# A hybrid encoder step: third weight buffer one trunk later, and the second half's MLP operands read whole from DRAM

## The chip, the cores and the metric

The kernel runs on one core of a Trainium2 chip. The metric is the device time of one execution in microseconds; the time before is the median of three runs. Five engines work side by side, each through its own list of instructions in order: PE (TensorE, matrix products), DVE (VectorE), ACT (ScalarE), POOL (GpSimd), and SP (SyncE), which here issues nearly all transfers (DMAs). An instruction that waits for a semaphore holds up everything behind it on its engine.

## The reference

One inference step of one layer of a streaming encoder with d = 1024, for 1024 prompt tokens and 32 sample tokens, all in float32:

```
h = rms_norm(x);  q,k,v,ch,cb,cc,ga,gb = split(h @ w_in)
a = window_attention(q,k,v) @ w_attn_out
b = (cb * conv3(cc * ch)) @ w_conv_out
x = x + (sigmoid(ga) * a + sigmoid(gb) * b) @ w_mix_out
x = x + memory_attention(rms_norm(x) @ w_cq) @ w_co        # 4 heads of 64, 256 memory rows
x = x + relu(rms_norm(x) @ w_up)**2 @ w_down               # hidden 4096
y = rms_norm(x)
```

The outputs are y, the last keys and values, the convolution's state and the memory keys and values.

## The kernel before, in words

Activations lie with features on the 128 partitions, in 8 blocks (f = 0 to 7), and tokens along the free axis. The 1056 tokens are cut into three chunks of 384, 384 and 288 (`CH`). A float32 product is made of three faster ones: each operand is split into a rounded high part and the remainder, and `gemm` (L193 to L195) adds wh·hi, wh·lo and wl·hi, 24 matmuls for a weight tile of 128x1024. `product` (L864 to L866) does the same for half a tile.

*Weights.* The program is a plan of items, each with the weight it needs. `fetch_w` (L155) issues the load of a raw tile on SP into one of two buffers named wr; if the dictionary `third` is filled, every third load goes to a buffer of another pool, so that three are in turn (the pool with tag ws behind the gate stage). `issue_w` then splits the tile: ACT casts it to wh (L129), DVE subtracts to get wl (L130). Items ask for their weights two ahead (`LOOK`). For the odd tiles of w_conv_out, w_mix, w_cq and w_co, which all three chunks use, wl is stored to DRAM as wl_d when first made (L172) and loaded back later (L166), so that only the cast is repeated.

*Stages around the change.* In the attention and gate stages POOL makes sums of weights in the tiles of the pool with tag ws and in xacc (`sum_step`: loads at L712, additions at L719, stores to gsum_d, wsum_d and usum_d at L723 and L725). `after_gates` (L1018) ends the gate stage; there `third` is filled. Then comes the trunk of each chunk: 8 items of w_conv_out (`do_conv_out`, L1042) and 8 of w_mix (`do_mix`, L1057). The first trunk carries one item more, the second trunk's first. The second trunk runs beside the first chunk's cross-attention, which uses w_cq, w_co and the memory keys (mkr, L1076). The third trunk is mixed with the MLP's first products.

*The MLP.* It works on halves of 528 tokens, and its `up` products on quarters of 264. `up_one(i, q)` (L1313) makes one product pair a and b of quarter q; the first half of the 24 matmuls goes to a, ACT copies a out of its accumulator (L1324), the second half goes to b, and DVE empties b (L1327, L1328). `put` and `flush` send the results to s_d and b_d (L1310). The operands of quarter 1 lie in `xa[1]`, in eight tiles named Z that `open_first` (L1221) opens; quarter 1 spans tokens 264 to 527, thus 120 tokens of the first chunk and 144 of the second. `normed(c, f)` (L1277) makes block f of chunk c of the MLP's normalised input in a ct buffer (there are six), and stores it to xn_d in DRAM (L1282). `second_split(f)` splits Z in place: ACT casts (L1296), DVE subtracts (L1297). `chunk_col` and `chunk_row` make the row R of scales for a chunk (DVE L240, PE L241 and L242, ACT L252), which the query products need when DVE takes them from their accumulators (L1109).

*What sets the order.* The list of fillers (`ones_q`, trunk items) and the table `at`, filled by `then(i, ...)`, say after which filler each call stands. The order on each engine is made by a scheduler from that program; only what is marked with `pin` keeps its place. So a DMA can be lifted far ahead of its place in the text, as far as its buffer allows in the scheduler's reckoning.

Of the kernel before, what the change touches and what calls it, by code (L numbers as in the profile page):

```python
# [10 lines left out]
F32 = mybir.dt.float32  # L11
# [11 lines left out]
CH = [(0, 384), (384, 384), (768, 288)]  # L23
NF = 8
HT = 528
QT = 264
# [14 lines left out]
def hybrid_step(ctx: ExitStack, tc: tile.TileContext, io):  # L41
    nc = tc.nc
    act, dve, pool_e, pe, sp = nc.scalar, nc.vector, nc.gpsimd, nc.tensor, nc.sync
# [7 lines left out]
    def opened(name, **kw):  # L51
        cm = tc.tile_pool(name=name, **kw)
        return cm, cm.__enter__()

    def closed(cm):
        cm.__exit__(None, None, None)
# [17 lines left out]
    def col(j):  # L74
        return prm[:, j : j + 1]
# [6 lines left out]
    xn_d = dram.tile([P, NF, NT], F32, name="xn_d")  # L82
# [14 lines left out]
    def pin(ins):  # L97
        return tc.keep_in_program_order(ins)
# [6 lines left out]
    def tmp(n, dt=F32):  # L105
        return tp.tile([P, n], dt, tag="ct", bufs=NCT, name=nm("ct"))
# [11 lines left out]
    def item(fn, *keys):  # L118
        plan.append((fn, keys))
        worder.extend(keys)  # L120
# [24 lines left out]
    third = {}  # L145
# [68 lines left out]
    def xacc_tile():  # L214
        xacc[0] = tp.tile([P, 1056], F32, tag="xacc", name=nm("xacc"))
        return xacc[0]
# [37 lines left out]
    def chunk_stats(c):  # L254
        chunk_col(c)
        chunk_row(c)
# [19 lines left out]
    W = {}  # L276
# [490 lines left out]
    def yslot(c):  # L767
        return slot(Y[c if c < 2 else "top"], f"Y{c}", CH[c][1])
# [22 lines left out]
    def pump(n):  # L791
        for into, at, t, get in coming:
            hi, lo = into[at] = (get(), get())
            pin(act.copy(hi, t))
            pin(dve.tensor_sub(lo, t, hi.bitcast(F32)))
        coming.clear()
        for into, at, src, cols, get in wanted[:n]:
            t = cols() if callable(cols) else tmp(cols)
            sp.dma_start(t, src)
            coming.append((into, at, t, get))  # L800
        del wanted[:n]
# [216 lines left out]
    def after_gates():  # L1018
        nonlocal m_cm, mpool, cr_cm, cr
        assert not pieces and "new" not in W  # L1020
        closed(x_cm)
        xacc_tile()
        third.update(n=0, pool=W["pool"])
        m_cm, mpool = opened("mpool", bufs=18, reuse_waits="tile")
        cr_cm, cr = opened("cross", bufs=1, reuse_waits="tile", side="right")

    item(after_gates)


# [73 lines left out]
    def do_cq(c, j):  # L1103
        def fn(w):
            n = CH[c][1]
            a = acc_tile([P, n])
            gemm(a, w, xc[c])
            t = tmp(n)
            dve.scalar_tensor_tensor(t, a, 0.125, R[c], op0=ALU.mult, op1=ALU.mult)  # L1109
            for e in range(2):  # L1110
                own, other = slice(64 * e, 64 * e + 64), slice(64 - 64 * e, 128 - 64 * e)
                q = yslot(c)
                act.copy(q[own], t[own])
                dve.tensor_sub(q[other], t[own], q[own].bitcast(F32))
                qc[2 * j + e, c] = q

        return fn
# [75 lines left out]
    def do_co(c, half):  # L1193
        def fn(w):
            n = CH[c][1]
            wh, wl = w
            fs = range(4 * half, 4 * half + 4)
            for f in fs:
                a = acc_tile([P, n])
                for k in range(2):  # L1200
                    s = slice(((f % 4) * 2 + k) * P, ((f % 4) * 2 + k) * P + P)
                    hi, lo = co[c][k]
                    pe.matmul(a, wh[:, s], hi, start=(k == 0), stop=False)
                    pe.matmul(a, wh[:, s], lo, start=False, stop=False)
                    pe.matmul(a, wl[:, s], hi, start=False, stop=(k == 1))
                x = x1[c][f]
                dve.tensor_add(x, a, x)
                if c and f > 4:
                    sq = tmp(n)
                    act.activation(sq, x, AF.Square)  # L1210
                    accs[c].append(sq)
                else:
                    square_acc(x, f, c)

        return fn
# [5 lines left out]
    def open_first():  # L1221

        closed(m_cm)
        S["l"] = ctx.enter_context(tc.tile_pool(name="first", bufs=4, reuse_waits="tile"))
        S["z"] = ctx.enter_context(tc.tile_pool(name="second", bufs=8, reuse_waits="tile"))
        for f in range(NF):
            z = zslot()
            xa[1][f] = (quarter(z, 0), quarter(z, 1))
            sp.dma_start(xa[1][f][1].bitcast(F32)[:, : CH[0][1] - QT], xn_d[:, f, QT : CH[0][1]])
        for name in ("w_cq", "w_co"):  # L1230
            del kept[name, 1]

# [26 lines left out]
    def zslot(dt=F32R):  # L1259
        return S["z"].tile([P, HT], dt, tag="Z", name=nm("Z"))  # L1260
# [14 lines left out]
    xa = [[None] * NF for _ in range(2)]  # L1275

    def normed(c, f):  # L1277
        t = tmp(CH[c][1])
        pin(dve.scalar_tensor_tensor(t, x1[c][f], col(G_MLP + f), R[c], op0=ALU.mult, op1=ALU.mult))
        o, n = CH[c]  # L1280
        if c < 2 or f > 3:
            sp.dma_start(xn_d[:, f, o : o + n], t)  # L1282
        if c == 1:
            sp.dma_start(xa[1][f][1].bitcast(F32)[:, CH[0][1] - QT :], t[:, : HT - CH[1][0]])
        if c == 2:
            top[f] = t
        if c == 0:
            hi, lo = (yslot(0)[:, :QT] for _ in range(2))
            xa[0][f] = (hi, lo)
            act.copy(hi, t[:, :QT])  # L1290
            pin(dve.tensor_sub(lo, t[:, :QT], hi.bitcast(F32)))

    def split_here(hi, lo):

        raw = lo.bitcast(F32)
        pin(act.copy(hi, raw))  # L1296
        pin(dve.tensor_sub(lo, raw, hi.bitcast(F32)))  # L1297

    def second_split(f):
        split_here(*xa[1][f])  # L1300
# [112 lines left out]
    def comb_split(kind):  # L1413
        for k in range(4):
            split_here(*comb[kind, k])
# [167 lines left out]
    def pump2(n):  # L1583
        for hi, lo in coming2:
            split_here(hi, lo)
        coming2.clear()
        for kind, k in wanted2[:n]:
            hi, lo = dn[kind, k] = dslots(kind, k)
            sp.dma_start(lo.bitcast(F32), op_d[kind][:, k])
            coming2.append((hi, lo))  # L1590
        del wanted2[:n]
# [8 lines left out]
    def cross_units(c):  # L1600
        units = [Cross(c, h) for h in ([0, 1, 2, 3] if c < 2 else [4, 0, 1, 2, 3])]
        nu = len(units)
        for i in range(nu + 2):
            calls = []
            if i < nu:
                calls.append(units[i].scores)
            if 0 <= i - 2 < nu:
                calls.append(units[i - 2].values)
            if 0 <= i - 1 < nu:
                calls.append(units[i - 1].turn)  # L1610
            yield ("call", calls)

    def cross_steps(c):

        steps = [("call", [mem_load if c == 0 else mem_load_s])]
        steps.append(("call", [lambda: chunk_stats(c)]))
        steps.append(("items", [(do_cq(c, j), ("w_cq", j)) for j in range(2)]))
        for i, step in enumerate(cross_units(c)):
            steps.append(step)
            if i < 4 - c:  # L1620
                steps.append(("call", []))
        if c:
            steps.append(("call", []))
        steps.append(("items", [(do_co(c, 0), ("w_co", 0))]))
        steps.append(("items", [(do_co(c, 1), ("w_co", 1))]))
        if c == 0:
            steps.append(("call", [lambda: chunk_stats(c)]))
        return steps

    def beside(steps, fillers, late=()):  # L1630
        for i, filler in enumerate(fillers):
            item(*filler)
            for x in [x for at, x in late if at == i]:
                item(lambda x=x: x())
            if steps:
                kind, what = steps.pop(0)
                for x in what:
                    if kind == "items":
                        item(*x)
                    else:  # L1640
                        item(lambda x=x: x())
        return steps
# [10 lines left out]
    trunks[0].insert(NF, trunks[1].pop(0))  # L1653
    left = beside([], trunks[0], [(i, lambda: pump(2)) for i in range(NF)])
    item(lambda: pump(0))
    left = beside(cross_steps(0), trunks[1])

    normeds = lambda c, at: [(at + f, lambda f=f: normed(c, f)) for f in range(NF)]
# [12 lines left out]
    def then(i, *what):  # L1671
        at.setdefault(i, []).extend(what)

    call = lambda fn, *args: lambda: item(lambda: fn(*args))
# [12 lines left out]
    assert opened_at == 18  # L1687
    then(18, call(open_first))
    for f in range(NF):
        then(19 + f // 4, call(normed, 1, f))  # L1690
        then(22, call(second_split, f))
    then(19, call(chunk_col, 2))
    then(20, call(chunk_row, 2))
# [291 lines left out]
```

## Time and profile before

| what | value |
|---|---|
| runs | 1779.01, 1780.84, 1780.94 us; median 1780.84 |
| profiled execution | 1778.09 us, span 1776.3 us from first to last instruction |
| mean granted TensorE clock | 0.990 |
| DVE, ACT, POOL busy | 67%, 48%, 32% of the span |
| bytes moved by DMA | 349.75 MB, mean 197 GB/s |
| gate stage | up to about 786 us |
| first trunk | about 810 to 884 us |
| quarter 1's operands | about 1072 to 1097 us |

The busy share of an engine is a mean over all stages, so a change is read from the stage it touches: there, which wait ends last. Waits of an engine other than PE cost nothing unless PE waits behind them. A row of the timeline gives start and duration in us, engine, line, operation, out<-in with shape, and in brackets the idle time before it with what ended it. In the view of stretches each engine has its busy us and number of instructions, then come the granted clock (1.00 is full speed), the DMA share and GB/s.

### The profile page before, as it was taken

How to read it: one execution, taken by the hardware profiler on the slowest of the kernel's cores; microseconds unless marked ns; L12 is line 12 of the kernel's file. 1: busy time of each engine (PE TensorE's matmuls, PEld its weight loads, DVE VectorE, ACT ScalarE, POOL GpSimd, SP SyncE). 2: the span in 40 equal slices, each digit the busy share in tenths (PEclk: the TensorE clock that was granted, in tenths of full speed). 3: DMA queues.
4: the chain of work that ended last, by engine and by line, in shares of the span. 5: the costliest groups of instructions: out<-in, count | busy, mean ns of one | idle time of the engine just before them, and what ended most of it. 6: DMA issues, size and time to landing. Idle time of an engine off the chain costs nothing.

```text
span 1776.3 us, 32569 instructions
## 1 busy us (share of the span) xinstructions
PE 1734.2 (98%) x12250; PEld 1716.3 (97%) x12250; DVE 1184.4 (67%) x2270; ACT 852.8 (48%) x1660; POOL 576.8 (32%) x651
## 2 busy tenths in 40 slices
PE   8999999999999999979999999999999999999998
PEld 8999999999999999979999989999999999999998
DVE  7776867868666647536667677786666686556575
ACT  8643534435335324324556665774444463333443
POOL 0025366543453444531225130004555510000121
PEclk9999999999999999989999998999999999999999
DMA  5333334333446888747765667575666686554554
GB/s 183 109 117 128 111 128 155 120 139 136 148 155 223 298 274 288 264 166 272 261 213 196 236 224 233 183 257 196 223 221 224 213 310 212 186 184 167 193 173 157
DMA packets 182221, 349.75 MB, mean 197 GB/s; under 512 B 19744, under 2 KB 102976, under 8 KB 181936
## 3 DMA queue, kind: packets, MB, share of 16 engines
q1 hardware_dynamic: 167008, 295.07, 49.1%
q0 software_dynamic: 15056, 52.60, 8.4%
q8 instruction: 96, 1.57, 0.4%
q14 instruction: 61, 0.50, 0.1%
HBM read 252.82 MB, written 94.19 MB: 195 GB/s over the span
## 4 chain that ended last, share of the span: by engine, by line
PE 77%; DMA 11%; POOL 6%; DVE 2%; issue 2%; ACT 2%; SPq 0%; DVEq 0%; POOLq 0%; ACTq 0%
PE acc L193 10%; PE acc L195 10%; PE acc L194 10%; PE acc L1772 6%; PE acc L1770 6%; PE acc L1771 6%; PE acc L864 5%; PE acc L866 5%; PE acc L865 5%; DMA wsum_d<-ws 3%; DMA wsum_d<-xacc 3%; POOL ws L719 2%; POOL xacc L719 2%; PE pc L864 2%; PE pc L865 2%
## 5 line engine op out<-in xcount | busy, mean ns | idle before, releaser
L129 ACT CAST wh<-wr 128x1024 fp32r<-128x1024 f32 x226 | 237.2, 1050 | 424.5 <-PE acc L1771 126.2
L130 DVE TENSOR_TENSOR wl<-wr,wh 128x1024 fp32r<-128x1024 f32 x226 | 292.5, 1294 | 140.6 <-ACT wh L129 138.6
L193 PE MATMUL acc<-X,wh 128*128 128x384 f32 (+1 forms) x864 | 281.8, 326 | 6.6 <-ACT wh L129 6.6
L194 PE MATMUL acc<-X,wh 128*128 128x384 f32 (+1 forms) x864 | 279.1, 323 | 0.0
L195 PE MATMUL acc<-X,wl 128*128 128x384 f32 (+1 forms) x864 | 278.5, 322 | 0.3 <-DVE wl L130 0.3
L269 POOL TENSOR_TENSOR xacc<-xacc,ct 128x384 f32<-128x384 f32 (+1 forms) x56 | 73.4, 1314 | 401.8 <-ACT ct L267 400.3
L193 PEld LDWEIGHTS acc<-X,wh 128*128 128x128 f32 x864 | 163.0, 189 | 7.2 <-ACT wh L129 6.6
L194 PEld LDWEIGHTS acc<-X,wh 128*128 128x128 f32 x864 | 163.1, 189 | 0.7
L195 PEld LDWEIGHTS acc<-X,wl 128*128 128x128 f32 x864 | 162.8, 188 | 0.9 <-DVE wl L130 0.8
L195 PE MATMUL acc<-Y,wl 128*128 128x384 f32 (+1 forms) x432 | 139.1, 323 | 1.8 <-DMA wl<-wl_d 1.8
L193 PE MATMUL acc<-Y,wh 128*128 128x384 f32 (+1 forms) x432 | 138.8, 323 | 0.4 <-ACT Y L774 0.4
L194 PE MATMUL acc<-Y,wh 128*128 128x384 f32 (+1 forms) x432 | 139.1, 322 | 0.0
L1770 PE MATMUL acc<-n,wh 128*128 128x264 f32 x352 | 100.2, 285 | 0.0
L1771 PE MATMUL acc<-n,wh 128*128 128x264 f32 x352 | 100.1, 284 | 0.0
L1772 PE MATMUL acc<-n,wl 128*128 128x264 f32 x352 | 100.0, 285 | 0.1
L129 ACT CAST PTh<-pt 128x512 fp32r<-128x512 f32 (+3 forms) x94 | 46.0, 516 | 111.6 <-PE pt L582 110.8
L719 POOL TENSOR_TENSOR ws<-ws 128x256 f32<-128x256 f32 x100 | 91.9, 919 | 5.6
L719 POOL TENSOR_TENSOR xacc<-xacc 128x256 f32<-128x256 f32 x100 | 87.9, 879 | 5.5 <-DMA xacc<-in_w_in 0.2
L195 PEld LDWEIGHTS acc<-Y,wl 128*128 128x128 f32 x432 | 81.1, 188 | 2.1 <-DMA wl<-wl_d 2.1
L193 PEld LDWEIGHTS acc<-Y,wh 128*128 128x128 f32 x432 | 80.9, 188 | 0.7 <-ACT Y L774 0.7
L194 PEld LDWEIGHTS acc<-Y,wh 128*128 128x128 f32 x432 | 81.1, 188 | 0.0
L864 PE MATMUL acc<-n,wh 128*128 128x264 f32 x256 | 72.9, 285 | 0.8 <-DVE Z L1502 0.8
(422 smaller groups left out, 5511.5 us busy)
## 6 DMA issues: line engine op xcount, KB each, us to landing
wr<-in_w_in SPq DMA_DIRECT2D x53, 512.0 KB, 3.7
wr<-in_w_up SPq DMA_DIRECT2D x53, 512.0 KB, 4.5
wr<-wsum_d SPq DMA_DIRECT2D x40, 512.0 KB, 3.4
wr<-in_w_conv_out SPq DMA_DIRECT2D x24, 512.0 KB, 4.3
wr<-in_w_mix SPq DMA_DIRECT2D x24, 512.0 KB, 4.8
wr<-in_w_down SPq DMA_DIRECT2D x24, 512.0 KB, 3.4
wl<-wl_d SPq DMA_DIRECT2D x18, 512.0 KB, 4.6
n_d<-Z SPq DMA_DIRECT2D x32, 264.0 KB, 4.3
```

The source lines that it names most:

```text
L129: act.copy(hi, src)
L130: dve.tensor_sub(lo, src, hi.bitcast(F32))
L193: pe.matmul(out, wh[:, a], hi, start=(k == 0), stop=False)
L194: pe.matmul(out, wh[:, a], lo, start=False, stop=False)
L195: pe.matmul(out, wl[:, a], hi, start=False, stop=(k == len(acts) - 1))
L719: pin(pool_e.tensor_tensor(t[:, to], t[:, x], t[:, y], op=ALU.add))
L864: pe.matmul(acc, wh[:, a], hi, start=(start and k == 0), stop=False, skip_group_check=True)
L865: pe.matmul(acc, wh[:, a], lo, start=False, stop=False, skip_group_check=True)
L866: pe.matmul(acc, wl[:, a], hi, start=False, stop=(k == 3), skip_group_check=True)
L1770: pe.matmul(a, wh[:, s], hi, start=(t == 0 and k == 0), stop=False, skip_group_check=True)
L1771: pe.matmul(a, wh[:, s], lo, start=False, stop=False, skip_group_check=True)
L1772: pe.matmul(a, wl[:, s], hi, start=False, stop=(t == 1 and k == 7), skip_group_check=True)
```

## The change

Two things are changed. First, `third` is no longer filled at the end of the gate stage, but by an item of its own behind the first trunk, so that the first trunk's loads take turns in two buffers. Second, the operands of quarter 1 are no longer put together from an early load of 120 columns (issued in `open_first`) and a copy of 144 columns out of each normalised tile; all eight `normed(1, f)` now stand at filler 19 (before, four at 19 and four at 20), and at filler 20 a new `second_load(f)` reads the 264 columns of each block from DRAM.

```
     def after_gates():
...
         xacc_tile()
-        third.update(n=0, pool=W["pool"])
...
     def open_first():
...
             xa[1][f] = (quarter(z, 0), quarter(z, 1))
-            sp.dma_start(xa[1][f][1].bitcast(F32)[:, : CH[0][1] - QT], xn_d[:, f, QT : CH[0][1]])
...
     def normed(c, f):
...
             sp.dma_start(xn_d[:, f, o : o + n], t)
-        if c == 1:
-            sp.dma_start(xa[1][f][1].bitcast(F32)[:, CH[0][1] - QT :], t[:, : HT - CH[1][0]])
...
+    def second_load(f):
+        sp.dma_start(xa[1][f][1].bitcast(F32), xn_d[:, f, QT:HT])
...
     left = beside([], trunks[0], [(i, lambda: pump(2)) for i in range(NF)])
     item(lambda: pump(0))
+    item(lambda: third.update(n=0, pool=W["pool"]))
     left = beside(cross_steps(0), trunks[1])
...
     then(18, call(open_first))
     for f in range(NF):
-        then(19 + f // 4, call(normed, 1, f))
+        then(19, call(normed, 1, f))
+    for f in range(NF):
+        then(20, call(second_load, f))
         then(22, call(second_split, f))
```

Line numbers of the changed kernel are lower by one from `after_gates` on, by two at `normed` and by four at `second_split` (L1292 and L1293 are its cast and subtraction, L1296 the new load), and by one again behind it.

What this does to the order on the engines is seen at three places. The first is on SP in the gate stage. A tile name with two numbers (wr_1614_9467) is a load into the third buffer; the other wr are the two usual ones.

```order
 L928 DMA ct_8899<-a_d_109 128x288
 L155 DMA wr_1518_8922<-in_w_in 128x1024
-L155 DMA wr_1614_9467<-in_w_conv_out 128x1024
+L155 DMA wr_1809_10255<-in_w_cq 128x1024
 L155 DMA wr_8974<-in_w_in 128x1024
 L920 DMA m_d_93<-ct_8837 128x384
```

The first load into the third buffer is another weight, from a later stage, in the same row. (The row above it, wr_1518_8922, is the gate stage's own third buffer, of another pool, which L933 switches on and L936 off; it is the same in both kernels.)

The second is on SP at the end of the first trunk. Before (mkr are memory keys, ct tiles the residual, wl_d the kept low halves):

```order
L155 DMA wr_1749_10025<-in_w_conv_out 128x1024
L1061 DMA ct_9903<-in_x 128x384
L1076 DMA mkr_12825<-in_cmem_k 64x256 x2
L155 DMA wr_10067<-in_w_conv_out 128x1024
L1061 DMA ct_9945<-in_x 128x384
L1076 DMA mkr_12832<-in_cmem_k 64x256 x2
L1061 DMA ct_9989<-in_x 128x384
L172 DMA wl_d_9987<-wl_9984 128x1024
L155 DMA wr_10109<-in_w_conv_out 128x1024
L166 DMA wl_10028<-wl_d_9259 128x1024
```

The same place in the changed kernel:

```order
L155 DMA wr_9981<-in_w_mix 128x1024
L1075 DMA mkr_12817<-in_cmem_k 64x256
L1060 DMA ct_9945<-in_x 128x384
L1075 DMA mkr_12817<-in_cmem_k 64x256
L155 DMA wr_10025<-in_w_conv_out 128x1024
L1060 DMA ct_9989<-in_x 128x384
L172 DMA wl_d_9987<-wl_9984 128x1024
L155 DMA wr_10067<-in_w_conv_out 128x1024
L1075 DMA mkr_12824<-in_cmem_k 64x256 x2
L166 DMA wl_10028<-wl_d_9259 128x1024
```

Every weight load stands where the next one stood before (10025 in the place of 10067, 10067 in that of 10109), as it does in the whole trunk from tile 9467 on: tile 9895 of w_mix stands where 9939 stood. Two loads of keys have moved in between the last weight load and the load of wl.

The third is where quarter 1's operands are made. On SP, before, the last twelve rows up to the next weight load (Z are the operands, b_d and s_d the spilled results):

```order
L1282 DMA xn_d<-ct_12578 128x384
L1284 DMA Z_12461<-ct_12578 128x144
L1282 DMA xn_d<-ct_12582 128x384
L1284 DMA Z_12463<-ct_12582 128x144
L1282 DMA xn_d<-ct_12586 128x384
L1284 DMA Z_12465<-ct_12586 128x144
L1282 DMA xn_d<-ct_12590 128x384
L1284 DMA Z_12467<-ct_12590 128x144
L1310 DMA b_d<-lt_12550 128x264
L1310 DMA s_d<-lt_12617 128x264
L1310 DMA b_d<-lt_12618 128x264
L155 DMA wr_12740<-in_w_up 128x1024
```

The same for the changed kernel; ahead of these rows stand six stores, a spill and the load of Z_12453:

```order
L1296 DMA Z_12454<-xn_d 128x264
L1296 DMA Z_12455<-xn_d 128x264
L1280 DMA xn_d<-ct_12518 128x384
L1296 DMA Z_12456<-xn_d 128x264
L1280 DMA xn_d<-ct_12521 128x384
L1296 DMA Z_12457<-xn_d 128x264
L1296 DMA Z_12458<-xn_d 128x264
L1309 DMA b_d<-lt_12550 128x264
L1296 DMA Z_12459<-xn_d 128x264
L1309 DMA b_d<-lt_12610 128x264
L1296 DMA Z_12460<-xn_d 128x264
L155 DMA wr_2383_12732<-in_w_up 128x1024
```

Stores and copies in turn have become loads between the last stores, with the next weight load still behind them all. On ACT, behind the last cast of Z, before:

```order
L1296 CAST Z_12467<-Z_12467 128x264
L252 COPY R_12594<-pr_12595 128x288
L129 CAST wh_12742<-wr_12740 128x1024
L1324 COPY lt_12789<-acc_12787 128x264
L129 CAST wh_12781<-wr_12779 128x1024
```

The same in the changed kernel:

```order
L1292 CAST Z_12460<-Z_12460 128x264
L129 CAST wh_12734<-wr_2383_12732 128x1024
L1323 COPY lt_12781<-acc_12779 128x264
L129 CAST wh_12773<-wr_12771 128x1024
L252 COPY R_12586<-pr_12587 128x288
```

The copy of R has moved from ahead of the first cast to behind the second.

More of the change, by code (lines that the diff above doesn't have):

```diff
@@ L1022, in after_gates @@
         xacc_tile()
-        third.update(n=0, pool=W["pool"])
         m_cm, mpool = opened("mpool", bufs=18, reuse_waits="tile")
@@ L1228, in open_first @@
             xa[1][f] = (quarter(z, 0), quarter(z, 1))
-            sp.dma_start(xa[1][f][1].bitcast(F32)[:, : CH[0][1] - QT], xn_d[:, f, QT : CH[0][1]])
         for name in ("w_cq", "w_co"):
@@ L1282, in normed @@
             sp.dma_start(xn_d[:, f, o : o + n], t)
-        if c == 1:
-            sp.dma_start(xa[1][f][1].bitcast(F32)[:, CH[0][1] - QT :], t[:, : HT - CH[1][0]])
         if c == 2:
@@ L1297, in split_here, with second_load @@
         pin(dve.tensor_sub(lo, raw, hi.bitcast(F32)))
+    def second_load(f):
+        sp.dma_start(xa[1][f][1].bitcast(F32), xn_d[:, f, QT:HT])
     def second_split(f):
@@ L1655, in hybrid_step @@
     item(lambda: pump(0))
+    item(lambda: third.update(n=0, pool=W["pool"]))
     left = beside(cross_steps(0), trunks[1])
@@ L1689, in hybrid_step @@
     for f in range(NF):
-        then(19 + f // 4, call(normed, 1, f))
+        then(19, call(normed, 1, f))
+    for f in range(NF):
+        then(20, call(second_load, f))
         then(22, call(second_split, f))
```

## The prediction

> **What bounds the kernel now.** The first view is the page: busy time by engine, then the slices with the granted TensorE clock.
>
> ```profile
> span 1776.3 us, 32569 instructions
> PE 1734.2 (98%) x12250; PEld 1716.3 (97%) x12250; DVE 1184.4 (67%) x2270; ACT 852.8 (48%) x1660; POOL 576.8 (32%) x651
> PEclk9999999999999999989999998999999999999999
> ```
>
> TensorE is busy for 1734.2 of 1776.3 us. Neither edit takes a matmul away, so only the 42 us in which it waits, and the stages at a lower clock (the two 8s), can move. The second view is the list of waits, TensorE alone.
>
> ```profile
> PE acc L864 <- ACT wh L129: 10.0, 2, 9.4
> PE acc L193 <- ACT wh L129: 6.6, 1, 6.6
> PE acc L864 <- ACT lt L1324: 2.3, 1, 2.3
> ...
> PE acc L195 <- DMA wl<-wl_d: 1.8, 1, 1.8
> PE acc L864 <- ACT lt L1354: 1.5, 1, 1.5
> PE acc L195 <- DVE wl L130: 1.5, 4, 0.5
> ```
>
> (A row has us in total, times, longest.) The 6.6 us are the start. Three others lie where the change reaches: the gate stage (9.4), the end of the first trunk (1.8), and the half-two `up` products (2.3). I take them in that order.
>
> **The change, part by part.** *The third buffer in the gate stage.* The chain of work that ended last, read around 776 us:
>
> ```profile
> 775.77 3.10 DMA usum_d<-ws
> 778.99 0.33 SPq L155
> 779.42 5.08 DMA wr<-in_w_in
> ...
> 785.70 0.69 PE acc L864
> ```
>
> SP's own waits in 750 to 800 us name the same releaser:
>
> ```profile
> SPq L155 <- DMA usum_d<-ws: 9.8, 1, 9.8
> ```
>
> The first weight load into the third buffer stands among the gate loads; it must wait until POOL's last partial sums have left that memory (778.9), and the w_in load behind it reaches DRAM only at 779.42. That is the 9.4 us. One would expect the change to remove it. But the order of the changed kernel has a third-buffer load in the same row, now w_cq, ahead of the same w_in load. The scheduler still lifts it. So I cost this at 0; the two ends are -9.4 (the stall goes) and 0.
>
> *Two buffers in the first trunk.* Each load there now stands where the next one stood. Is a loop of two buffers fast enough? From 809 to 884 us, the landing of the weight loads, the group of casts, one subtraction and TensorE's last rows:
>
> ```profile
> DMA to landing us min/median/max: 3.8/4.9/6.1
> ```
> ```profile
> L129 ACT CAST wh<-wr 128x1024 fp32r<-128x1024 f32 x16 | 16.7, 1046 | 7.0 <-DMA wr<-in_w_conv_out 5.5 <-PE acc L194 1.5
> ```
> ```profile
> 859.74 1.23 DVE L130 TENSOR_TENSOR wl<-wr,wh 128x1024 fp32r<-128x1024 f32 x1 [0.53 <-ACT wh L129]
> ```
> ```profile
> 882.41 0.33 PE L193 MATMUL acc<-Y,wh 128*128 128x384 f32 x1
> 882.58 0.34 PE L194 MATMUL acc<-Y,wh 128*128 128x384 f32 x1
> 884.69 0.45 PE L195 MATMUL acc<-Y,wl 128*128 128x384 f32 x1 [1.77 <-DMA wl<-wl_d]
> ```
>
> A buffer is held for landing 4.9 + cast 1.05 + subtraction 1.23 = 7.2 us. Matmuls start every 0.17 us, so an item of 24 takes 4.2 and two items 8.3. There are 1.1 us to spare per pair of loads. The tightest item is the 15th (w_mix, tile 9895): its buffer comes free when the subtraction above ends, 860.97. What stood there before shows what it gets:
>
> ```profile
> L155 SPq DMA_DIRECT2D wr<-in_w_mix x1: 424/424/424, 861.4 to 861.4; - x1
> ...
> DMA to landing us min/median/max: 5.6/5.6/5.6
> ```
>
> Landed at 867.0, cast at 868.1, subtracted at 869.3. TensorE begins the kept product at 882.4, so this item three items of 4.2 before that, and earlier by the waits among them (0.5 at most, the last row of the list of waits): 869.3 to 869.8. It needs the low half two matmuls on, 0.35 later. Between 0.3 and 0.8 us remain, so I take 0. The other end is a loop that is always late: with the longest landing, 6.1, and 0.7 us of queueing on ACT and DVE, a pair takes 9.1 against 8.3, times 7 pairs, +5.6.
>
> *What is behind it on SP.* The stall at 884.69 waits for a kept low half out of DRAM. SP around it:
>
> ```profile
> 878.84 0.43 SPq L155 DMA_DIRECT2D wr<-in_w_conv_out  x1
> 879.31 0.79 SPq L166 DMA_DIRECT2D wl<-wl_d  x1
> ```
>
> In the changed order two key loads stand between these two rows. The trace has them elsewhere, and the nearest SP issue of a small tile is the removed one:
>
> ```profile
> L1229 SPq DMA_DIRECT2D Z<-xn_d x8: 382/384/423, 1071.9 to 1075.3; - x8
> ```
>
> Two of these are 0.8 us, nothing covers it, as TensorE waits for exactly this load: the stall becomes 2.6, **+0.8** (ends: 0, if SP catches up, and +0.8).
>
> *The operands.* Eight early loads (8 x 0.384, some 3.8 us of SP with the gaps) and eight copies go; eight loads of 264 columns come, each behind the landing of its own store. SP's first rows here, then the landing times of the weight loads and of the stores:
>
> ```profile
> 1078.00 0.38 SPq L155 DMA_DIRECT2D wr<-in_w_up  x1
> 1078.47 0.44 SPq L1282 DMA_DIRECT2D xn_d<-ct  x1
> ```
> ```profile
> DMA to landing us min/median/max: 3.4/4.3/5.7
> ```
> ```profile
> L1282 SPq DMA_DIRECT2D xn_d<-ct x8: 437/552/865, 1078.5 to 1088.1; - x8
> ...
> DMA to landing us min/median/max: 2.1/4.0/5.8
> ```
>
> The first new load waits on SP for the first store, issued at 1078.47 and landed 5.8 later: 1084.2. In that wait the rest of the stores, two spills and the next weight load are queued behind it. From there twelve issues follow ahead of the weight load (8 loads at about 0.45, 2 stores at 0.55, 2 spills at 0.39: 5.5 us), so that it leaves at 1089.7. Before, it left here:
>
> ```profile
> 1090.86 0.94 SPq L155 DMA_DIRECT2D wr<-in_w_up  x2
> ```
>
> It leaves 1.2 us earlier. Who waits for it? ACT first, and TensorE behind ACT:
>
> ```profile
> 1091.51 0.40 ACT L252 COPY R<-pr 128x288 f32<-128x288 f32 x1 [0.45 <-PE pr L242]
> 1095.14 1.04 ACT L129 CAST wh<-wr 128x1024 fp32r<-128x1024 f32 x1 [3.23 <-DMA wr<-in_w_up]
> 1096.09 0.37 ACT L1324 COPY lt<-acc 128x264 f32<-128x264 f32 x1
> ```
> ```profile
> 1096.52 0.59 PE L864 MATMUL acc<-Z,wh 128*128 128x264 f32 x1 [2.27 <-ACT lt L1324]
> ```
>
> The copy that empties the accumulator stands behind a cast whose weights have not landed; TensorE waits 2.27 us. The order keeps copy behind cast, so TensorE goes on at 1095.3: **-1.2**. But R's copy, ahead of both at 1091.51, now stands behind two casts, and DVE's two scalings that need R and free the two query accumulators stand behind two subtractions:
>
> ```profile
> L130 DVE TENSOR_TENSOR wl<-wr,wh 128x1024 fp32r<-128x1024 f32 x5 | 6.1, 1223 | 0.7 <-ACT wh L129 0.7
> ...
> L1109 DVE SCALAR_TENSOR_TENSOR ct<-acc,R 128x288 f32<-128x288 f32 x2 | 0.8, 450 | 0.0
> ```
>
> The second cast ends at 1096.4, its subtraction at 1097.6, the first scaling at 1098.05; TensorE has by then ended its 12 matmuls (1095.3 + 1.45 = 1096.75) and wants that bank: **+1.3**. Net +0.1.
>
> What is not fixed is the clock. In stages (busy time of each engine, then the granted clock):
>
> ```profile
> 1092.30:1095.70 3.40, 1.60 (x11) 1.39 (x11) 3.40 (x10) 0.56 (x1) 0.00 (x0) 1.00 0.99 295
> 1095.70:1102.50 6.80, 5.99 (x27) 5.99 (x28) 5.75 (x9) 4.48 (x8) 0.00 (x0) 0.50 0.79 284
> ```
>
> After a stretch of 3.4 us with TensorE busy for 1.60, the clock is 0.50 for 6.8 us, which costs 3.4 us at most. [...] I leave it as it is, and take -4.6 (-1.2 and -3.4) and +3.0 (+1.3 and +1.7) as ends.
>
> [...]
>
> *The rest.* Placements shift in the third chunk's cross-attention and the later `up` products, and 8 of 24 DMAs fewer run there. The longest wait there is the 1.5 for L1354 in the list of waits, so I take 0, with 1.5 either way. **Sum:** 0 + 0 + 0.8 + 0.1 + 0 = +0.9 us. The profiled execution took 1778.09 (span 1776.3 and 1.8 around it), so it would take 1779.0; the median of the runs is 1780.84, 2.75 above it, so the forecast for the median is 1780.84 + 0.9 = **1781.7 us**.
>
> **The rivals.** *The two-buffer loop bounds the first trunk (slower).* Place: 810 to 884 us. It decides from the point where landing plus queueing passes 8.3 - 2.3 = 6.0 us on average; 4.9 of landing speaks against it, the half us left at the 15th item and landings up to 6.1 speak for it. Price +5.6 over the forecast: 1787.3.
>
> *SP and DVE stand behind the stores (slower).* There are six ct buffers, so the seventh normalised tile waits on DVE for the first store:
>
> ```profile
> 1084.51 0.62 DVE L1279 SCALAR_TENSOR_TENSOR ct<-Gb,prm,R 128x384 f32<-128x384 f32 x1 [1.21 <-DMA Z<-ct]
> ```
>
> In the changed kernel this tile stands ahead of the step that empties an accumulator and of the subtraction for the second query product. If the store lands after about 1085, TensorE waits there some 1 to 2 us, and one more stretch of 3.4 us falls to half clock: +1.7 + 1.7 = 3.4 on top: 1785.1.
>
> *The stall at 1096.52 and its half clock go (faster).* The weight load leaves earlier, R comes in time: the +1.3 is not paid and 3.4 are saved, 0.9 - 1.3 - 3.4 = -3.8: 1777.0. For it speaks SP's freer queue, against it the order of R's copy.
>
> *The change does what its name says in the gate stage (faster).* The 9.4 go, and the half clock behind them (785.7 to 791.9) with 3.1: 1769.2. The order speaks against it.
>
> **How the numbers follow.** Forecast 0.46, two-buffer loop 0.20, stores 0.16, half clock gone 0.14, gate stall gone 0.04. Outside 1776 to 1788.5 lie the last, some of the half clock and the longest loop, about 0.15, and inside are the bounds of the operands (1777.1 to 1784.7). 0.2% is 3.6 us, about what a measurement can tell from no change: same is 1777.3 to 1784.4. Faster 0.18, same 0.46, slower 0.36.
>
> **What would show it.** In the gate stage a 9.4 us wait for wh again, with SP's L155 behind usum_d. In the first trunk no wait for wh over 0.5 us, and the wait for wl_d near 2.6. At 1090 SP's next weight load about a us earlier, a wait under 2 us behind the copy of L1323, then one of about 1.3 behind DVE's L1108. Wrong would be waits for wh at several items of the first trunk, a waiting query product at 1085 to 1089, or a clock of 1.00 throughout 1092 to 1103.

## The result and the profile after

The changed kernel takes 1780.48 us in the median of 12 runs (1778.03 to 1784.92); the kernel before, run beside it, 1778.89 us (12 runs, 1771.96 to 1781.58). The ratio over the runs is 1.0016 with a 95% interval of 1.0006 to 1.0025: some 2.8 us slower (the two medians lie 1.6 us apart), inside the 0.2% that the prediction called no change. The profiled execution has a span of 1779.8 us.

The list of TensorE's waits (us in total, times, longest) answers to the one of before:

```profile
PE acc L864 <- ACT wh L129: 9.6, 1, 9.6
PE acc L193 <- ACT wh L129: 7.3, 1, 7.3
PE acc L864 <- ACT lt L1323: 3.7, 1, 3.7
PE acc L195 <- DMA wl<-wl_d: 2.5, 1, 2.5
```

All four are there again. The gate stall stays at 9.6, the wait for wl_d is 2.5 instead of 1.8, and the wait behind the copy out of the accumulator is 3.7 instead of 2.3, where I had it shorter. The gate stage on SP and POOL, with start, duration and operation:

```profile
776.53 1.45 POOL L723 DMA_DIRECT2D usum_d<-ws  x2 [0.41 <-POOL ws L719]
```
```profile
753.76 0.33 SPq L155 DMA_DIRECT2D wr<-in_w_in  x1
780.37 0.33 SPq L155 DMA_DIRECT2D wr<-in_w_cq  x1
780.80 0.38 SPq L155 DMA_DIRECT2D wr<-in_w_in  x1
```
```profile
787.29 0.69 PE L864 MATMUL acc<-X,wh 128*128 128x384 f32 x1 [9.56 <-ACT wh L129]
```

SP issues nothing from 754 to 780: it stands at the load of w_cq into the third buffer, at first for POOL's loads into that memory (15.4 us) and at last for POOL's last store (9.8 us). The w_in load that TensorE needs is the next row.

In the first trunk the 15th item's cast, its subtraction and the matmul that needs it, then the wait for wl_d and the stretches around that and around the operands (in the view of stretches the granted clock follows POOL's column):

```profile
869.08 1.05 ACT L129 CAST wh<-wr 128x1024 fp32r<-128x1024 f32 x1 [4.38 <-DMA wr<-in_w_mix]
870.17 1.23 DVE L130 TENSOR_TENSOR wl<-wr,wh 128x1024 fp32r<-128x1024 f32 x1
871.45 0.44 PE L195 MATMUL acc<-M,wl 128*128 128x384 f32 x1
```
```profile
886.66 0.45 PE L195 MATMUL acc<-Y,wl 128*128 128x384 f32 x1 [2.46 <-DMA wl<-wl_d]
```
```profile
883.80:887.20 3.40, 0.94 (x6) 0.62 (x5) 0.00 (x1) 1.04 (x1) 0.00 (x0) 1.00 0.89 339
887.20:890.60 3.40, 3.40 (x13) 3.40 (x12) 2.72 (x5) 2.64 (x5) 1.33 (x1) 0.50 0.35 102
...
1098.80:1102.20 3.40, 0.00 (x0) 0.00 (x0) 0.70 (x2) 1.75 (x4) 0.00 (x0) 1.00 1.02 373
1102.20:1105.60 3.40, 3.36 (x15) 3.37 (x16) 3.24 (x5) 1.50 (x3) 0.00 (x0) 0.51 0.67 230
```

A stretch at half clock now follows the wait for wl_d (0.50 from 887.2 to 890.6), where there was none before; the one behind the copy is 3.4 us long instead of 6.8. Quarter 1's operands, on SP, ACT and PE; below SP's rows the landing of the first of these weight loads, and the landing of the same load in the kernel before (it left there at 1090.9):

```profile
1094.84 0.32 SPq L1296 DMA_DIRECT2D Z<-xn_d  x1
1095.21 0.94 SPq L155 DMA_DIRECT2D wr<-in_w_up  x2
```
```profile
DMA to landing us min/median/max: 5.6/5.6/5.6
```
```profile
DMA to landing us min/median/max: 4.2/4.2/4.2
```
```profile
1100.86 1.04 ACT L129 CAST wh<-wr 128x1024 fp32r<-128x1024 f32 x1 [1.48 <-DMA wr<-in_w_up]
1101.81 0.37 ACT L1323 COPY lt<-acc 128x264 f32<-128x264 f32 x1
```
```profile
1102.24 0.59 PE L864 MATMUL acc<-Z,wh 128*128 128x264 f32 x1 [3.75 <-ACT lt L1323]
```

The weight load leaves behind the last operand load and lands 5.6 us later; the copy stands behind its cast, and TensorE behind the copy.

### The profile page after: what moved, and what is told of

Read it like the earlier page. It is cut to its first block, busy times and chain, and to the rows that moved or that the text cites. A ratio compares the mean times of both kernels' runs of the same rounds, so it can differ in the third digit from the quotient of the medians.

```text
span 1779.8 us, 32541 instructions
## 1 busy us (share of the span) xinstructions
PE 1734.9 (97%) x12250; PEld 1717.8 (97%) x12250; DVE 1186.2 (67%) x2270; ACT 854.0 (48%) x1660; POOL 572.9 (32%) x651
## 3 DMA queue, kind: packets, MB, share of 16 engines
HBM read 253.41 MB, written 94.19 MB: 195 GB/s over the span
## 5 line engine op out<-in xcount | busy, mean ns | idle before, releaser
L1772 PE MATMUL acc<-n,wh 128*128 128x264 f32 x352 | 100.2, 285 | 0.0
L1773 PE MATMUL acc<-n,wh 128*128 128x264 f32 x352 | 100.2, 285 | 0.0
L568 ACT ACTIVATE S<-S,nmx 128x257 f32<-128x257 f32 (+1 forms) x132 | 64.2, 488 | 20.9 <-DVE nmx L563 20.5
```

The lines of the kernel that those rows point to most:

```text
L1772: pe.matmul(a, wh[:, s], hi, start=(t == 0 and k == 0), stop=False, skip_group_check=True)
L1773: pe.matmul(a, wh[:, s], lo, start=False, stop=False, skip_group_check=True)
```

## The experiments

TensorE issues the same number of matmuls in all kernels, so the time between the starts of the n-th and the m-th can be set side by side; the stretches below are made so, one profile each. *Trunk* is from the 5090th to the 5600th (810 to 902 us before), *cross* from there to the 6750th (1080), *operands* to the 7000th (1118), *later* to the 8000th (1251). A profile is one execution, so it is the groups that count.

| kernel | third from | operands | pin | trunk | cross | operands | later |
|---|---|---|---|---|---|---|---|
| before | gate stage | copies | no | 92.05 | 178.62 | 37.35 | 133.13 |
| e0 | gate stage | copies | no | 92.85 | 178.24 | 36.62 | 132.63 |
| after | trunk 2 | SP | no | 94.87 | 180.47 | 36.52 | 131.54 |
| e1 | trunk 2 | copies | no | 94.19 | 177.98 | 35.87 | 131.39 |
| e2 | gate stage | SP | no | 95.66 | 180.88 | 38.82 | 130.77 |
| e3 | trunk 2 | SP | yes | 94.92 | 178.46 | 38.81 | 131.32 |
| e4 | gate stage | copies | yes | 94.25 | 180.84 | 37.11 | 128.51 |
| e5 | trunk 2 | POOL | no | 92.00 | 177.28 | 36.64 | 128.40 |
| e6 | trunk 2 | SP, twice | no | 91.40 | 180.09 | 41.55 | 128.03 |
| e7 | never | SP | no | 92.78 | 178.95 | 40.12 | 133.01 |
| e8 | trunk 2 | copies | yes | 92.42 | 177.90 | 36.37 | 131.20 |
| e9 | gate stage | SP | yes | 97.90 | 178.81 | 37.79 | 132.68 |
| e10 | trunk 2 | POOL | yes | 93.53 | 177.16 | 38.62 | 126.22 |
| e11 | gate stage | POOL | yes | 96.01 | 180.76 | 35.98 | 128.15 |

My theory after the comparison of the two profiles was that the first edit made the whole difference, since TensorE loses 2.8 us in the first trunk (92.05 to 94.87) and nothing on balance in the three stretches behind it (+1.85, -0.83, -1.59). The rival was the second edit.

**e1, the first edit alone.**

```
@@ before
     def after_gates():
-        third.update(n=0, pool=W["pool"])
...
     item(lambda: pump(0))
+    item(lambda: third.update(n=0, pool=W["pool"]))
```

> The first edit alone: third is filled behind the first trunk, the operands are made as before. Theory 1 (the first edit made the +0.16%: two buffers in the first trunk): ratio to before 1.0009 to 1.0018; in the profile the waits at 853 to 863 us and the wl wait of about 2.5 us are there, with a stretch at clock 0.50 behind it, TensorE is 2.5 to 3 us later at 900 us than before, counted from 811 us; the wait behind the copy of L1323 stays near 2.3. Theory 2 (the operands made it): ratio 0.9995 to 1.0004, and TensorE no later than 0.8 us at 900.

Measured: 1776.65 us against 1777.89 for the kernel before, ratio 0.9993 (0.9980 to 1.0006). The theory falls. Its list of waits has the two that were to tell:

```profile
PE acc L864 <- ACT lt L1323: 2.1, 1, 2.1
...
PE acc L195 <- DMA wl<-wl_d: 1.9, 1, 1.9
```

The wait for wl_d is 1.9, not 2.5. In the profile theory 1 is not all wrong: a stretch at half clock follows that wait (3.41 us from 885.0), and the trunk takes 94.19, 2.1 us more than before. But the three stretches behind it are shorter by 3.9 together, and the runs show no loss.

**e2, the second edit alone.** The changed kernel, with `third` filled in `after_gates` as before.

```
@@ after
     def after_gates():
+        third.update(n=0, pool=W["pool"])
...
-    item(lambda: third.update(n=0, pool=W["pool"]))
```

> The second edit alone: third is filled at the end of the gate stage as before, the operands are loaded whole behind their stores. Theory 1 (the first edit made the slowdown): ratio 0.9993 to 1.0004; the wait behind the copy of L1324 is near 3.7 us instead of 2.3, but is paid back by a shorter stretch at half clock. Theory 2 (the operands made it): ratio 1.0008 to 1.0018.

Measured: 1779.48 us, ratio 1.0012 (0.9999 to 1.0025). This is the side of theory 2, though the interval still takes in 1. The wait behind the copy is larger yet, and the clock is 0.50 for 6.83 us from 1102.71:

```profile
1104.35 0.59 PE L864 MATMUL acc<-Z,wh 128*128 128x264 f32 x1 [5.29 <-ACT lt L1324]
```

The first trunk takes 95.66 here with its third buffer in place, more than in the changed kernel without it. A stretch at half clock follows the wait for wl_d here too (from 887.7). So the 2.8 us of the first pair of profiles were no mark of the edit.

**e0, the kernel before once more.** No edit.

> The kernel before once more, unchanged, as a measure of the spread. Ratio 0.9992 to 1.0008. In a second profile the waits of TensorE stay within 0.3 us each. [...]

Measured: 1777.42 against 1778.02 us, ratio 1.0000 (0.9983 to 1.0017): an interval as wide as the difference to be explained. Its waits at the three places are those of before (9.7, 1.8 and 2.3), and yet the stretches at half clock are others: one at 1030.4 that before had not, 3.4 us instead of 6.8 behind the copy, none at 1164. Two profiles of one kernel differ by up to 0.8 us in a cell of the table. Two kernels that differ by the second edit alone differ by more, even where that edit changes nothing: e4 and e9 (below) issue the same instructions in the same order on every engine in the trunk, and take 94.25 and 97.90 there.

**e3 and e4, the lifted load pinned.** `pin` keeps the first load into the third buffer in its place in the program, in the changed kernel (e3) and in the kernel before (e4).

```
     def fetch_w():
...
-        sp.dma_start(raw.rearrange("p (i c) -> p i c", i=4) if len(src.shape) == 3 else raw, src)
+        put_w = pin if third and third["n"] == 3 and third["pool"] is W.get("pool") else (lambda x: x)
+        put_w(sp.dma_start(raw.rearrange("p (i c) -> p i c", i=4) if len(src.shape) == 3 else raw, src))
```

> The changed kernel, with the first load into the third buffer pinned to its place in the program, so that the scheduler does not lift it into the gate stage. Theory 3 (this lifted load, held by POOL's last stores, is the 9.6 us gate stall on SP): the stall falls below 2 us and the half clock behind it goes too, 1767 to 1772 us, ratio to before 0.993 to 0.996. Rival (the w_in load behind it would wait for its own buffer, or the next wait in the gate stage takes its place): the gain is under 3 us, ratio 0.998 to 1.001.

> The kernel before, with the same one load pinned to its place in the program. Theory 3: the gate stall falls from 9.4 to below 2 us with the half clock behind it, 1765 to 1770 us, ratio 0.992 to 0.995, some 2 to 3 us below the changed kernel with the pin (the third buffer still serves the first trunk). Rival: gain under 3 us, ratio 0.998 to 1.001.

Measured: e3 1768.06 us (6 runs, 1767.28 to 1770.43), ratio 0.9950 (0.9930 to 0.9970); e4 1767.74 us (9 runs), ratio 0.9945 (0.9926 to 0.9963). Theory 3 holds, and both beat both kernels. SP in e3 (its lines are one higher): the w_in loads leave at 752 to 755, and nothing stands at POOL's stores.

```profile
751.98 2.80 SPq L156 DMA_DIRECT2D wr<-in_w_in  x2
...
757.14 0.33 SPq L156 DMA_DIRECT2D wr<-gsum_d  x1
```
```profile
765.00:778.00 13.00, 13.00 (x83) 13.00 (x82) 8.10 (x12) 4.95 (x7) 11.51 (x14) 1.00 0.70 242
778.00:790.00 12.00, 12.00 (x80) 12.00 (x79) 4.07 (x7) 2.25 (x4) 0.37 (x1) 1.00 0.52 166
```

TensorE is busy throughout at clock 1.00. From the 4800th to the 5090th matmul it takes 46.42 us against 58.30 in the changed kernel: 9.56 of wait, and the other 2.3 I put down to the half clock behind it (the 4.3 us at 0.50 from 787.29 to 791.63 come to 2.2). The 2 to 3 us that I expected between e3 and e4 are not there (0.3).

**e5, the operand loads on POOL's queue.**

```
     def second_load(f):
-        sp.dma_start(xa[1][f][1].bitcast(F32), xn_d[:, f, QT:HT])
+        pool_e.dma_start(xa[1][f][1].bitcast(F32), xn_d[:, f, QT:HT])
```

> The changed kernel with the eight operand loads issued by POOL's queue instead of SP's. Theory 4 (the second edit's cost is the up-weight load that is behind these loads on SP and lands late): the weight load leaves some 4 us earlier, the 3.7 us wait behind the copy of L1323 falls under 1.5, and the time is 2 to 5 us under the changed kernel, ratio to before 0.9985 to 1.0000. Rival (the operands themselves come late, the weight load does not matter): TensorE waits for Z instead, by 2 us or more, ratio 1.001 to 1.003.

Measured: 1772.66 us (1760.09 to 1777.26), ratio 0.9971 (0.9944 to 0.9997), more than theory 4 wanted. The waits at the operands:

```profile
1079.77 0.39 PE L865 MATMUL acc<-Z,wh 128*128 128x264 f32 x1 [0.44 <-DVE Z L1293]
1081.76 0.39 PE L865 MATMUL acc<-Z,wh 128*128 128x264 f32 x1 [0.86 <-DVE Z L1293]
1083.91 0.53 PE L864 MATMUL acc<-Z,wh 128*128 128x264 f32 x1 [1.28 <-ACT lt L1323]
```

The wait behind the copy is 1.28; the operands themselves come late, as the rival had it, but only by 1.3 together. A part of the gain is something else. The profiled execution took 1760.11 us; four of the 12 runs lie at 1760.1 to 1765.0 and the other eight at 1771.0 to 1777.3, so it is one of the short ones. It has no gate stall, with the lifted load in place:

```profile
766.20 1.45 POOL L723 DMA_DIRECT2D usum_d<-ws  x2 [0.41 <-POOL ws L719]
```
```profile
770.04 0.33 SPq L155 DMA_DIRECT2D wr<-in_w_cq  x1
770.48 0.38 SPq L155 DMA_DIRECT2D wr<-in_w_in  x1
```

POOL was 10 us earlier in this execution, so SP was free at 770 instead of 780. The gate stall is a race between POOL's sums and TensorE. Over the unpinned profiles that have the lifted load:

| profile | POOL's last store landed | TensorE waits |
|---|---|---|
| before, e0, after, e1, e2 | 778.9, 781.5, 780.2, 778.9, 779.0 | 9.4, 9.7, 9.6, 9.6, 8.1 |
| e6 | 773.5 | 1.6 |
| e5 | 769.9 | none |

In the pinned kernels it lands at 782 to 787, later than in any of these, and TensorE does not wait. Why POOL is early in some executions stays open.

**e6, the operand loads twice.** The line of `second_load` stands twice.

> The changed kernel with each operand load issued twice, to double the suspected cost. Theory 4: eight issues of 0.4 us and 1.06 MB more stand ahead of the weight load, the wait behind the copy of L1323 grows from 3.7 to 7 or 8 us, ratio to before 1.0035 to 1.006. Rival (these loads lie beside other work): within 0.0006 of the changed kernel, 1.001 to 1.0022.

Measured: 1779.81 us against 1778.02, ratio 1.0006 (0.9987 to 1.0024). By its time alone the rival; but the profiled execution, 1771.87 us, is one of the two short ones of 12 (the others lie at 1776.7 to 1781.3), and it has a gate stall of only 1.6. In it the operands' stretch is 41.55 us, 5.0 over the changed kernel's and 3.1 over the mean with single loads, in two waits, of which the later one is at the expected place, released by the cast itself, and the earlier one is for the bank that the query product holds:

```profile
1091.32 0.39 PE L864 MATMUL acc<-Z,wh 128*128 128x264 f32 x1 [2.78 <-DVE ct L1108]
1098.20 0.59 PE L864 MATMUL acc<-Z,wh 128*128 128x264 f32 x1 [3.70 <-ACT wh L129]
```

So in this profile the loads stand on the path there. The ten longer runs, with a median of 1779.9, show no price for the doubled loads against the changed kernel's 1780.48. As a price for the whole kernel the run settles nothing.

**e7, no third buffer at all behind the gate stage.** The item that fills `third` is taken out of the changed kernel.

```
@@ after
-    item(lambda: third.update(n=0, pool=W["pool"]))
```

> The changed kernel with no third buffer behind the gate stage at all: two buffers for the rest of the program. Theory 5 (two buffers are enough, and the lifted third load only costs): the 9.6 us gate stall goes as with the pin, the waits for wh in the trunks stay under 1 us each, ratio to before 0.993 to 0.9965. Rival (the later trunks with the cross-attention beside them need the third buffer): the gate stall goes but 5 us or more come back as waits for wh at 890 to 1250 us, ratio 0.997 to 1.002.

Measured: 1770.10 us, ratio 0.9968 (0.9948 to 0.9988), between the two. The gate stall is gone, the first trunk takes 92.78, but a wait of 3.9 for wh is at the operands, and the last two stretches are among the longest. Two buffers do in the first trunk; at the short `up` products, which ask for a weight each, these numbers speak for a third.

**e8 to e11, all with the pin,** to see the edits without the race: e8 is e1 with the pin, e9 is e2, e10 is e5, and e11 is e9 with the loads on POOL.

> The first edit alone with the pinned load, so that POOL's timing no longer decides. Theory 6 (the first edit costs nothing): within 1.0 us of the kernel before with the pin (1767.7), ratio to before 0.9937 to 0.9950. Rival (the first trunk's two-buffer loop and the later load of wl cost the 0.8 us or more of the forecast): 1768.6 to 1770.

> The second edit alone with the pinned load. Theory 7 (the second edit costs 1 to 2 us at 1090, where the weight load lands late): 1768.7 to 1770, and the wait behind the copy of L1324 is 3.5 to 5.5 us against about 2 with the old operands. Rival (it costs nothing on the whole): within 0.7 us of 1767.7.

> The changed kernel with the pinned load and the operand loads on POOL's queue. Theory 7: 2 to 3 us under the changed kernel with the pin (1768.1), 1765 to 1766.5, ratio 0.9925 to 0.9940, with the wait behind the copy of L1323 under 1.5 us. Rival (the gain of the loads on POOL was only the gate stage's luck): 1767.5 to 1769.

> The third buffer for the first trunk as before, the pinned load, and the operand loads on POOL's queue. If the first edit costs nothing it is within 1 us of the run with the third buffer late and the loads on POOL; if the two-buffer loop costs something it is 1 to 2 us below it, the fastest of all, at 1764 to 1765.

Measured: medians, with the ratio to the kernel before and its interval.

| third from | copies | loads on SP | loads on POOL |
|---|---|---|---|
| gate stage | e4 1767.74, 0.9945 (0.9926 to 0.9963) | e9 1774.81, 0.9992 (0.9975 to 1.0008) | e11 1766.52, 0.9938 (0.9917 to 0.9959) |
| trunk 2 | e8 1768.56, 0.9948 (0.9931 to 0.9966) | e3 1768.06, 0.9950 (0.9930 to 0.9970) | e10 1763.50, 0.9923 (0.9902 to 0.9944) |

With the copies, the first edit costs 0.8 us in the medians (1768.56), inside theory 6's bound and at the foot of the rival's, and nothing that the intervals could tell. With loads on SP or on POOL the same edit gains, 6.8 and 3.0 us. The second edit costs 7.1 us in the upper row and -0.5 in the lower. Theory 7 wanted 1 to 2 in the upper, and its price is missed on the high side. In e9 the wait behind the copy (L1325 there) is as expected:

```profile
PE acc L194 <- ACT wh L129: 10.1, 5, 8.0
PE acc L865 <- ACT lt L1325: 4.2, 1, 4.2
```

but over e4 it loses 3.7 us in the trunk, where the order is the same, and 4.2 in the later stretch, and gains 2.0 in the one called cross; that the profiles don't explain. (With the third buffer early, the pin puts the load of tile 9467 behind that of 9573, and TensorE waits 1.2 us at 822.8, in e11 1.6; e4 waits 0.5 there.) The loads on POOL gain in both rows, 4.6 and 8.3 us over SP, though in e10 1.9 us of wait behind the copy are left where I expected under 1.5. Little of this gain lies at the late weight load: in the mean of e5, e10 and e11 the operands' stretch takes 37.1 us against 38.4 with loads on SP (after, e2, e3, e7, e9), but the later stretch 127.6 against 131.9, with 4.1 us of idle TensorE time in it against 6.0. The order on the engines differs there, and which part of it gains was not tested. e10 is the fastest kernel of the study, 0.77% below the kernel before; e11 is 3.0 us above it, which neither side of its expectation had, so the early third buffer brings nothing there either.

## Why the prediction was right, point by point

The forecast of 1781.7 us and +0.9 us stands against 1780.48 and +0.16% (0.06 to 0.25), some 2.8 us. The sign and the order of size were right. Term by term the sum was less good, and that it came so near is in part luck: the +0.8 did not hold in other runs, and neither part of the operands' +0.1 (-1.2 and +1.3) came.

*The gate stall, taken as 0.* Right, for the reason given: another third-buffer load in the same row, the same wait. e3 and e4 show that this load is the cause. What I had not seen is that the stall depends on when POOL ends, and that in some executions it is short or absent with the same order.

*Two buffers in the first trunk, taken as 0.* Right, but closer than forecast. The 15th weight was expected to land at 867.0, and its cast began as it landed, at 869.1, in a profile that stands 0.8 us later at the trunk's start. Its subtraction ended at 871.40 and the matmul that needs it began at 871.45: of the margin of 0.3 to 0.8 us nothing was left, and TensorE has no wait of 0.25 us or more for it. Over all profiles without a third buffer in the first trunk, that stretch takes 93.3 us in the mean (eight profiles: after, e1, e3, e5 to e8, e10), against 93.5 for the three with it and without the pin (before, e0, e2).

*The load of wl behind two more, +0.8.* In the profile after it is +0.7 (1.77 to 2.46), as worked out. But it did not hold as a price: without the early third buffer the wait is 1.9 in e1, 2.2 in e3, 1.4 in e5, 0.5 in e6, 0.8 in e7 and e8 and 1.2 in e10, and in most of these it is no longer than before. One reason could be that a wait for a transfer that doesn't itself wait for TensorE is shorter by whatever TensorE lost shortly before; no run tests this. And the half clock behind it in the profile after (3.4 us at 0.50, so 1.7 us at most) was not in the sum.

*The operands, +0.1.* Here a step failed: "so TensorE goes on at 1095.3: -1.2". The weight load left as forecast: TensorE is 5.44 us later there (the second query product starts at 1093.42 instead of 1087.98), so 1095.21 is 1089.77 on the old scale, against 1089.7. That fits so well by luck: the first store landed after 4.52 us and not 5.8, so the first load left at 1088.29, 1082.85 on the old scale, where I had 1084.2; and the twelve issues from there to the weight load took 6.9 us, where I had 5.5. But the mechanism, the weight load behind them all, was right. It was the landing that I took over unchanged, 4.2 us; behind eight loads just issued, of 132 KB each, it was 5.55, and the wait grew to 3.75. The other profiles agree: this weight load lands in 4.0 to 4.5 us with copies (before, e0, e1, e4, e8) and in 5.6 to 7.1 with loads on SP (after, e2, e3, e7, e9). That the loads just ahead cause this is read from the order; it was not tested apart from the rest of the edit. Nor did the +1.3 for R's late copy come: no wait of 0.25 us or more follows until 1151; the long wait and the half clock probably gave DVE the time. In this pair of profiles the longer wait doesn't even lengthen the stretch, 36.52 us against 37.35, as the half clock behind it is 3.4 us shorter. In the mean of five profiles each, the operands' stretch takes 36.7 us with copies and 38.4 with loads on SP, and the three last stretches together 346.8 (345.2 to 349.1) and 349.8 (348.5 to 352.1): +3.0, of which 1.7 at the operands, against 0.1 forecast. (Without e7, which has no third buffer, the +3.0 are 2.5.) These sums are a hint and no more: between the same two groups the trunk, which this edit does not reach, differs by 2.1 us (93.2 and 95.2). No run shows the +1.7 in the upper end, for half clock that lasts 3.4 us longer (the price of the rival with the stores has one such term too): at the operands the clock was 0.50 for 6.8 us before and for 3.4 in e0, both behind a wait of 2.3, for 3.4 in the profile after behind 3.75 and for 6.83 in e2 behind 5.29.

*What is shown and what is not.* By the runs alone: first edit 0.9993 (0.9980 to 1.0006), second 1.0012 (0.9999 to 1.0025), both 1.0016 (1.0006 to 1.0025). The runs alone can't part the two edits. With the stretches, the slowdown probably lies with the second edit, and the longer landing of the weight load is one cause that every profile with loads on SP bears out; that it is the whole cause is not shown. The loads on POOL, which let the weight load go ahead, gain, but mostly in a later stretch. Why the second edit costs so differently with the pin (7.1 and -0.5) stays open.

*The rivals.* The one with SP behind the stores did not come: DVE's wait for the first store was 0.49 us, nobody waited for it, and the wait that grew is another, behind the landing of the weight load. The two-buffer loop did not bind. The half clock behind the copy did not go, it fell from 6.8 us to 3.4, as it did in e0 without any edit. The gate stall's end, priced at -12.5, was no part of this change, but the price was good: its stretch falls from 58.95 us before to 46.42 in e4.

## What to carry to other kernels

A load that a scheduler lifts into an early stage because its buffer seems free can hold the whole queue behind it (here SP's, for 9.8 us at POOL's last store); look for the row at which the issuing engine stands longest, and pin that row before tuning what lies behind it. When a transfer moves, cost its landing anew from what was issued just ahead of it, not only its leaving (here 5.6 us instead of 4.2). And a difference of 2 to 3 us between two profiles means little where stretches of half clock and a race between engines shift by themselves (e4 and e9 take 94.25 and 97.90 us for one order): profile the same kernel twice first, and look at a stretch that the edit cannot reach.

## What the runs showed of the hardware

A wait at one place was followed by half clock in one profile and not in two others. In the profile after, TensorE is idle for 2.46 us between 883.80 and 887.20, and the clock is 0.50 from 887.20 to 890.60 (above). In e0, 1.76 us of idle time at this place leave it at 1.00:

```profile
883.60:887.00 3.40, 1.64 (x9) 1.33 (x9) 1.19 (x1) 0.00 (x0) 0.10 (x1) 1.00 1.00 371
887.00:890.40 3.40, 3.40 (x21) 3.40 (x21) 1.18 (x2) 1.97 (x3) 1.02 (x1) 1.00 1.02 410
```

Before, the wait there is 1.77 us (up to 884.69), and the clock is 1.00 from 880.70 to 887.50. It was also at 0.50 behind a stretch without a wait: from 1061.60 to 1065.00 in the kernel before TensorE is busy for 3.40 of 3.40 us at clock 1.00, with 22 of its 32 matmuls the column sums pq (L224, 128x1, 250 ns in the median), and from 1065.00 to 1068.40 the clock is 0.50. What brings the clock down in one of these cases and not in another is not shown.
